# A decoder layer with sparse attention: the DMA issues of the projections in written order, ScalarE's searches served first by VectorE, and tile 2's search held back to the attention

## The chip, the cores and the metric

The kernel runs on one core of a Trainium2 chip. The metric is the device time of one execution in microseconds (us). Engines are named as the profile names them: PE is TensorE (matrix products), PEld its weight loads, DVE is VectorE, ACT is ScalarE, POOL is GpSimd, and SP is the engine whose queue issues all DMAs here.

## What is computed

One decoder layer for 1024 tokens of width 1024, all in f32:

```
mod = silu(c) @ w_mod + b_mod -> shift1, scale1, gate1, shift2, scale2, gate2
h   = x * (1 + scale1) + shift1
q, k, v, u, iq, ik, iw = split(h @ w_in)      # q, k, iq, ik get rotary positions
score[t, s] = sum over 8 indexer heads of iw * relu(iq . ik / 8), s <= t
attn  = for each token: softmax attention over the 256 keys of highest score, 8 heads of 64
pool  = trailing means of u (windows 2, 4, 8, 16) minus u, times w_pool, times pool_scale
x = layer_norm(alpha * x + gate1 * (concat(attn, pool) @ w_o))
h = x * (1 + scale2) + shift2
x = layer_norm(alpha * x + gate2 * swiglu(h))
```

## The kernel before

The tokens are eight tiles of 128 (tile i holds tokens 128 i to 128 i + 127). The matrix products of the projections split each f32 operand into a high and a low part and take three products (`SPLITS`), so every weight block is loaded raw (`raw_R`, three slots), copied by ACT (high part), and subtracted by POOL or DVE (low part) into `ws_W`.

The work runs in stages, one after the other on PE:

- **Index projection** (up to 82 us in the profile): iq, ik.
- **Score stage** (82 to 182 us): for tiles 2 to 7 PE multiplies (`lg`), ACT takes the relu (`relu_K`), DVE multiplies by iw and adds (`score_X`). The q projection's products (`pj`) are pieces put between them. Its results get their rotary positions on POOL in a ring of three buffers (`rope_V`) and are stored to memory (`q_d`).
- **u, k and v projections** (182 to 371 us), 24 groups of 24 products (`pair`, `pj`). Among the first eight groups stand the remaining four rows of the modulation: 16 loads of 1 MB (`mset_K`, three buffers), products with `silb` (`md`), a copy by ACT into `macc_V`, and `mod_fin`, which sums it (`gt`, `mc`). The two `macc_V` buffers lie over the ring `rope_V`, so the first copy waits until the last q tile has been stored. The gate's bias and sum lie in `grow`, one half row at a time.
- **Attention** (371 to 524 us): units of a pair of heads and a tile, tiles from 7 down to 0. PE makes the logits (`s`), DVE adds the mask of the search and takes the maximum in one pass (`sm_H` from `s` and `score_X`), ACT takes the exponential, POOL normalises, PE transposes (`pT`) and multiplies by v (`o`).
- **Output projection, feed-forward and second norm** (524 us to the end).

Which 256 keys a token takes is found by a **search** by bits over the scores: 15 passes over the high 16 bits, 16 passes over the low ones, and a final part that writes the mask over the scores. `bisect` is that search as a generator that yields before each step the engine and an estimated duration. Tiles 5 and 4 together and tile 3 (`TILES_A`) run their passes on ACT, with begin, middle and final part on DVE (`colsA_X`, buffers `junkA_T`, `junkB_X`); tiles 7 and 6 together (`colsD_X`) and tile 2 (`colsE_X`, keys in `keysA_X`, `LATE = [2]`) run on DVE alone. Tile 2's mask is needed when tile 2's first unit is reached, in the third of the four groups of tiles.

Two things set the order. The framework's scheduler may move an instruction ahead of earlier written ones of the same engine, except where `keep_in_program_order` is called on it. The kernel has its own model of the times (`Times`, `Queue`): every instruction goes through a `Queue`, and before an instruction is written whose engine is idle in the model, `fill` writes steps of open searches into the gap. From the first `open_stream` to the end of the v projection the set `pinned` holds V, A and G (DVE, ACT, POOL): these engines keep the written order. SP and PE don't, and in the attention none does. `fill` leaves tile 2 alone as long as the search of tiles 7 and 6 is open, so tile 2's search is written in the attention.

Of the kernel before, what the change touches and what calls it, by code (L numbers as in the profile page):

```python
# [18 lines left out]
ALU = mybir.AluOpType  # L19

P = 128
S = 1024
# [14 lines left out]
TILES_A = [[3], [5, 4]]  # L37
# [7 lines left out]
LATE = [2]  # L45
# [28 lines left out]
def f_(ap):  # L74

    return ap.bitcast(F32)
# [54 lines left out]
class Queue:  # L131
# [24 lines left out]
    def __getattr__(self, op):  # L156
        f = getattr(self.eng, op)

        def call(*a, **k):
            tm = self.times  # L160
            aps = [x for x in list(a) + list(k.values()) if hasattr(x, "tensor")]
            outs = aps[:1] + ([k["accum_out"]] if "accum_out" in k else []) + ([a[-1]] if op == "tensor_tensor_reduce" else [])
            ins = aps[1:]
            if self.name == "S":
                at = tm.ready("S", outs, ins)
                tm.dma = max(tm.dma, at) + outs[0].nbytes() / 320e3
                tm.done("S", outs, ins, tm.dma + 2.0)
                return f(*a, **k)
            if tm.fill is not None:
                tm.fill(self, tm.ready(self.name, outs, ins))  # L170
            ins_ = f(*a, **k)  # L171
            if aps:
                at = max(self.t, tm.ready(self.name, outs, ins))
                self.t = at + self.cost(op, aps, k)
                tm.done(self.name, outs, ins, self.t)
            if self.name in self.pinned:
                self.tc.keep_in_program_order(ins_)
            return ins_

        return call  # L180
# [3 lines left out]
def decoder_layer_kernel(  # L184
# [7 lines left out]
    pinned, times = set(), Times()  # L192
    V, A, G, T, SP = (Queue(tc, e, n, pinned, times) for e, n in
                      ((nc.vector, "V"), (nc.scalar, "A"), (nc.gpsimd, "G"), (nc.tensor, "T"), (nc.sync, "S")))
# [13 lines left out]
    def buf(where, off, n, name, dt=F32):  # L208
        return nc.alloc_sbuf_tensor_at(f"{name}_{where}{off}", [P, n], dt, offset=area[where] + 4 * off).ap()
# [13 lines left out]
    def psA(nm="pa"):  # L223
        return ps_tile(ps1, "ps1", 512, 4, nm)
# [44 lines left out]
    def raw_slot():  # L269
        n_raw[0] += 1  # L270
        return RAW[(n_raw[0] - 1) % 3]

    def split(dst, raw, n, lo_eng=None):
        A.activation(dst[:, 0:n], raw, AF.Copy)
        (lo_eng or V).tensor_tensor(dst[:, n : 2 * n], raw, f_(dst[:, 0:n]), ALU.subtract)
# [140 lines left out]
    def q_flush(keep):  # L416
        while len(q_spill) > keep:
            t, raw = q_spill.pop(0)
            SP.dma_start(q_d[t], raw)
# [10 lines left out]
    gate_d = [tc.dram_tile([1, 1024], F32, name=f"gate{q}_d") for q in range(2)]  # L430
# [228 lines left out]
    streams = []  # L659

    def open_stream(*a):
        pinned.update(PIN)
        b = bisect(*a)
        streams.insert(0, [T.t, next(b), b, a[0]])
        times.fill = fill

    def start(st):
        return max(st[0], queues[st[1][0]].t)

    def advance(st):  # L670
        fill, times.fill = times.fill, None
        q = queues[st[1][0]]
        try:
            st[1] = next(st[2])
        except StopIteration:
            streams.remove(st)
        st[0] = q.t
        times.fill = fill

    def need(i):  # L680
# [3 lines left out]
    def fill(q, until):  # L684
        while True:

            first = [st for st in streams if 7 in st[3]]
            todo = [st for st in streams if not (first and st[3] == LATE) and st[1][0] == q.name and start(st) + st[1][1] <= until + SLACK.get(q.name, 0.0)]
            if not todo:
                return  # L690
            advance(min(todo, key=start))


    n_rr = [0]
# [2 lines left out]
    def q_piece():  # L697
        if not qt[2]:
            if qt[0] >= NT:
                return  # L700
            qt[1], qt[2] = proj_pieces(qt[0])
        qt[2].pop(0)()
        if not qt[2]:
            qpend.append((qt[0], qt[1]))
            qt[0] += 1

    for i in range(2, NT):
# [3 lines left out]
        n = P * (i + 1)  # L711
# [33 lines left out]
    wps = buf("X", 7552, 1024, "wps", F32R)  # L745
# [63 lines left out]
        A.activation(vst[t // 4][:, t % 4], v3(pp), AF.Copy)  # L809

    MSET = [buf("K", 2048 + i * 2048, 2048, "mset") for i in range(3)]
    silb = buf("X", 5312, 256, "silb")
    grow = buf("X", 5568, 512, "grow")
    macc = [buf("V", 5616 + i * 512, 512, "macc") for i in range(2)]
    m_ps = {}

# [18 lines left out]
    def mod_fin(s_):  # L835

        row, c = divmod(s_, 2)
        acc = macc[s_ % 2]
        if row in (0, 3):
            pm = psA("gt")  # L840
            T.matmul(pm, ones, acc, start=True, stop=True)
            V.tensor_tensor(grow[0:1, :], grow[0:1, :], pm[0:1, :], ALU.add)
            SP.dma_start(gate_d[row // 3][:, c * 512 : (c + 1) * 512], grow[0:1, :])
            if s_ != 7:
                n = {0: 1, 1: 6, 6: 7}[s_]
                SP.dma_start(grow[0:1, :], bg_in[n // 6 : n // 6 + 1, n % 2 * 512 : n % 2 * 512 + 512])
        else:
            pc = psA("mc")
            for j in range(4):
                T.matmul(pc[:, j : j + 1], acc[:, j * P : (j + 1) * P], ones[:, 0:1], start=True, stop=True)  # L850
            u = (row - 1) * 8 + c * 4
            V.tensor_tensor(m2[:, u : u + 4], pc[:, 0:4], bcol[:, 16 + u : 20 + u], ALU.add)
            if s_ == 5:
                V.scalar_tensor_tensor(h2c[:, 0:8], m2[:, 8:16], 1.0, lnc[:, 0:8], ALU.add, ALU.mult)
                V.scalar_tensor_tensor(h2c[:, 8:16], m2[:, 8:16], 1.0, lnc[:, 8:16], ALU.add, ALU.mult)
                V.tensor_tensor(h2c[:, 8:16], h2c[:, 8:16], m2[:, 0:8], ALU.add)

    def w_loads(w_in):
        for kp in range(3):
            raws[kp] = raw_slot()  # L860
            SP.dma_start(raws[kp], w_in[kp])
        raws[3] = w_in
# [10 lines left out]
    def at_(slot, f):  # L873
        late.setdefault(slot, []).append(f)

    while qt[2] or qt[0] < NT:
        q_piece()
    w_loads(wu_in)
    for h in range(3):
        mod_load(h)  # L880
    SP.dma_start(lnc, lncol_in)
    SP.dma_start(grow[0:1, :], bg_in[0:1, 0:512])
    V.tensor_copy(silb.rearrange("p (k r) -> p k r", r=32), silc.unsqueeze(2).to_broadcast([P, 8, 32]))
    for i in range(4):
        G.memset(ub[i][:, 0:16], 0.0)
# [4 lines left out]
        q_evac(*qpend.pop(0))  # L890
    wp_raw = raw_slot()
    SP.dma_start(wp_raw[:, 0:512], wpool_in)
    split(wps, wp_raw[:, 0:512], 512)
    at_(1, lambda: q_flush(0))

    def u_f(g, c):
        return lambda pp, ks: mm_k(pp, lambda k, b: ww(k, b, g * P, P), lambda k, a: hh(k, a, c * 512, 512), ks)
# [11 lines left out]
    held, pair = {}, None  # L909
    for n_, (kind, a, b) in enumerate(groups):  # L910
        if n_ in PAIRS:
            pb = psB("pair")
            held[n_], held[n_ + 1] = pb[:, 0:512], pb[:, 512:1024]
            pair = [(held[q_], u_f(*groups[q_][1:]) if kind == "u" else t_f(groups[q_][1])) for q_ in (n_, n_ + 1)]
        if n_ in held:
            for kp in range(2):
                for pp, f in pair:
                    f(pp, [4 * (n_ not in PAIRS) + 2 * kp, 4 * (n_ not in PAIRS) + 2 * kp + 1])
        else:
            held[n_] = psA("pj")  # L920
            (u_f(a, b) if kind == "u" else t_f(a))(held[n_], range(KT))
        pp = held[n_]
        if n_ in (6, 14):
            w_loads(wk_in if n_ == 6 else wv_in)
        if n_ in (7, 8, 15, 16):
            for kp in ((0, 1) if n_ % 2 else (2, 3)):
                w_split(kp)
        nd = n_ + 2 if n_ in PAIRS else n_ + 1
        if kind == "u":
            at_(nd, lambda a=a, b=b, pp=pp: u_take(a, b, pp))  # L930
            if b == 1:
                at_(nd + 1, lambda a=a: u_split(a))
                at_(nd + 1, lambda a=a: u_split2(a))
                at_(nd + POOL_AT, lambda a=a: u_pool(a))
        elif kind == "k":
            tr = n_ + (4 if n_ in PAIRS or n_ - 1 in PAIRS else 3)
            at_(nd, lambda a=a, pp=pp, tr=tr: take(a, pp, tr))
        else:
            at_(nd, lambda a=a, pp=pp: v_take(a, pp))
        if n_ == 20:  # L940
            SP.dma_start(GR, gate_d[0].to_broadcast([P, 1024]))
        q_ = n_ - MOD_AT
        if 0 <= q_ < 9:
            if q_:
                mod_fin(q_ - 1)
            if q_ < 8:
                mod_half(2 * q_)
        for f in late.pop(n_, []):
            f()
        if 0 <= q_ < 8:  # L950
            mod_half(2 * q_ + 1)
# [777 lines left out]
    for p in range(1, NFP):  # L1729
        n_of = {"g": 0, "d": 0, "u": 0}  # L1730
        for kind in DOWN_AT if p < NFP - 1 else "g" * 7 + "u" * 7:
            n = n_of[kind]
# [133 lines left out]
```

## Time and profile before

| what | value |
|---|---|
| runs | 1308.19, 1311.80, 1307.18 us; median 1308.19 |
| profiled execution | 1309.66 us; its span 1307.9 us, granted clock 0.964 |
| PE busy | 1211.9 us (93%) |
| DVE busy | 1001.6 us (77%) |
| ACT busy | 650.4 us (50%) |
| POOL busy | 718.7 us (55%) |

The shares are means over stages with different limits. The span begins with the first instruction that the profiler sees; the execution's own time holds 1.8 us more. In the rows below a time in square brackets is how long the engine stood idle before the instruction, with what ended the wait; "x16" is a count of instructions that stand behind one another; L171 is the line of the `Queue` helper through which nearly all instructions pass, so rows are told apart by tiles.

### The profile page before, as it was taken

To read this page: it belongs to the slowest core of one execution; us is meant where nothing else is said; L and a number is where in the kernel's file an instruction comes from. 1 tells how busy PE (TensorE), PEld (TensorE's weight loads), DVE (VectorE), ACT (ScalarE), POOL (GpSimd) and SP (SyncE) were. 2 spreads that over 40 slices of the span, in tenths; PEclk is the share of its full clock that TensorE was granted. 3 is DMA by queue.
4 is the path that set the end of the run, shared out by engine and by line. 5 is a ranking of instruction groups with operands and counts; after the bars stand their busy time and mean duration, and the time that the engine had idled before them with its cause. 6 is when DMAs were issued, how large, how long until landed. Compare 5 with 4: busy or idle time off the path is not lost.

```text
span 1307.9 us, 16418 instructions
## 1 busy us (share of the span) xinstructions
PE 1211.9 (93%) x5622; PEld 936.8 (72%) x5622; DVE 1001.6 (77%) x1846; ACT 650.4 (50%) x1343; POOL 718.7 (55%) x509
## 2 busy tenths in 40 slices
PE   7979895999988899998789999999999999999996
PEld 5755563677865566887678787878788787878775
DVE  6769999799847666567797777776878777777698
ACT  3346784665897888356534333333424333333531
POOL 1382263467313246237767475574838475576848
PEclk8989998999988999999799999999999999999999
DMA  9510043740100015500121111212010111203112
GB/s 350 196 68 17 17 161 126 267 171 30 44 17 9 9 41 178 177 9 10 54 75 33 65 65 33 81 33 81 33 65 33 65 65 33 81 33 114 49 58 119
DMA packets 32468, 103.40 MB, mean 79 GB/s; under 512 B 3577, under 2 KB 3577, under 8 KB 28801
## 3 DMA queue, kind: packets, MB, share of 16 engines
q1 hardware_dynamic: 32384, 102.36, 22.4%
q8 instruction: 44, 0.72, 0.2%
q14 instruction: 40, 0.32, 0.1%
HBM read 92.90 MB, written 9.45 MB: 78 GB/s over the span
## 4 chain that ended last, share of the span: by engine, by line
PE 55%; DVE 24%; ACT 7%; POOL 6%; issue 6%; DMA 1%; SPq 0%; DVEq 0%; POOLq 0%; ACTq 0%
PE gu L171 24%; PE dn L171 14%; DVE junk_X L171 4%; PE wo L171 4%; DVE score_X L171 4%; PE pj L171 3%; PE s L171 2%; DVE act_W L171 2%; PE pair L171 2%; PE pT L171 2%; PE o L171 2%; POOL wraw_R L171 2%; DVE stat_C L171 1%; DVE utmp_X L171 1%; DVE hr_H L171 1%
## 5 line engine op out<-in xcount | busy, mean ns | idle before, releaser
L171 PE MATMUL gu<-hr_H,wblk_T 128*128 128x512 f32 (+1 forms) x924 | 218.3, 389 | 4.9 <-POOL wblk_T L171 1.9
L171 PE MATMUL gu<-hr_H,wblk_V 128*128 128x512 f32 (+1 forms) x924 | 215.1, 384 | 3.7 <-POOL wblk_V L171 1.9
L171 PEld LDWEIGHTS gu<-hr_H,wblk_T 128*128 128x128 f32 x924 | 173.0, 192 | 41.5 <-POOL wblk_T L171 3.6
L171 PEld LDWEIGHTS gu<-hr_H,wblk_V 128*128 128x128 f32 x924 | 170.0, 188 | 40.0 <-POOL wblk_V L171 3.6
L171 DVE TENSOR_TENSOR res_X<-res_X,dn 128x512 f32<-128x512 f32 (+1 forms) x253 | 159.0, 678 | 15.4 <-PE dn L171 15.3
L171 PE MATMUL pj<-ws_W,hT_H 128*128 128x512 f32 x456 | 118.4, 409 | 7.2 <-POOL ws_W L171 5.1
L171 POOL TENSOR_TENSOR wraw_R<-wraw_R 128x512 f32<-128x512 f32 x64 | 94.7, 1487 | 47.0 <-DVE wblk_T L171 23.7
L171 POOL TENSOR_TENSOR wraw_W<-wraw_W 128x512 f32<-128x512 f32 x60 | 86.6, 1452 | 57.9 <-DVE wblk_V L171 29.3
L171 POOL TENSOR_SCALAR sm_H<-sm_H,stat_X 128x1024 f32<-128x1024 f32 (+7 forms) x64 | 49.7, 791 | 116.7 <-DVE stat_X L171 106.1
L171 PEld LDWEIGHTS pj<-ws_W,hT_H 128*128 128x128 f32 x456 | 85.7, 194 | 32.1 <-issue 6.8
L171 PE MATMUL dn<-wblk_T,act_W 128*128 128x512 f32 x324 | 79.6, 394 | 4.5 <-DVE act_W L171 4.5
L171 PE MATMUL dn<-wblk_V,act_W 128*128 128x512 f32 x324 | 78.5, 391 | 2.9 <-DVE act_W L171 2.5
L171 DVE TENSOR_SCALAR_CACHE_REDUCE junk_X<-keysD_T,colsD_X 128x1024 int16<-128x1024 int16 (+1 forms) x64 | 78.9, 1267 | 0.2
L171 ACT ACTIVATE wblk_V<-wraw_R 128x512 fp32r<-128x512 f32 x56 | 35.2, 629 | 80.6 <-POOL wraw_R L171 62.2
L171 PEld LDWEIGHTS dn<-wblk_T,act_W 128*128 128x128 f32 x324 | 60.8, 189 | 19.2 <-DVE act_W L171 6.6
L171 POOL TENSOR_TENSOR ws_W<-raw_R,ws_W 128x1024 fp32r<-128x1024 f32 x17 | 44.6, 2643 | 53.8 <-ACT ws_W L171 53.8
L171 PEld LDWEIGHTS dn<-wblk_V,act_W 128*128 128x128 f32 x324 | 60.4, 188 | 17.4 <-DVE act_W L171 4.2
L171 ACT ACTIVATE wblk_V<-wraw_W 128x512 fp32r<-128x512 f32 x53 | 33.1, 627 | 75.0 <-POOL wraw_W L171 56.4
L171 ACT ACTIVATE wblk_T<-wraw_W 128x512 fp32r<-128x512 f32 x56 | 35.0, 628 | 66.3 <-POOL wraw_W L171 50.2
L171 ACT ACTIVATE wblk_T<-wraw_R 128x512 fp32r<-128x512 f32 x52 | 32.5, 627 | 61.0 <-POOL wraw_R L171 45.6
L171 ACT ACTIVATE junkA_T<-keys_T,colsA_X 128x768 bf16<-128x768 uint16 (+3 forms) x62 | 54.3, 876 | 5.8 <-DVE colsA_X L171 5.2
L171 ACT ACTIVATE utmp_X<-gu 128x512 f32<-128x512 f32 x33 | 19.7, 598 | 73.4 <-PE gu L171 73.4
(295 smaller groups left out, 2769.5 us busy)
## 6 DMA issues: line engine op xcount, KB each, us to landing
mset_K<-in_wmr_dram SPq DMA_DIRECT2D x16, 1024.0 KB, 6.0
wm_K<-in_wma_dram SPq DMA_DIRECT2D x16, 512.0 KB, 9.7
wraw_R<-in_wg_dram SPq DMA_DIRECT2D x6, 1024.0 KB, 4.8
wraw_R<-in_wd_dram SPq DMA_DIRECT2D x12, 512.0 KB, 3.5
wraw_W<-in_wup_dram SPq DMA_DIRECT2D x12, 512.0 KB, 3.6
wraw_R<-in_wup_dram SPq DMA_DIRECT2D x10, 512.0 KB, 3.8
wraw_W<-in_wg_dram SPq DMA_DIRECT2D x5, 1024.0 KB
wraw_W<-in_wd_dram SPq DMA_DIRECT2D x10, 512.0 KB, 3.6
```

The source lines that it names most:

```text
L171: ins_ = f(*a, **k)
```

## The change

It has three parts that touch the same stages.

1. **SP in written order.** `Queue` calls `keep_in_program_order` on DMAs too, and `"S"` is added to `pinned` after the last q piece, until the end of the v projection. With it the written order is changed: all q stores stand ahead of the modulation's later loads (`q_flush(0)` at once, no longer in a later slot), the loads of wk and wv stand four groups earlier (`n_ in (2, 10)`), the low part of the pooling weights (`wps`) is subtracted by POOL and no longer by DVE, and the gate's row is loaded, summed and stored whole (`grow` of 1024, two stores and two loads in place of four and four; `silb` moves to another area to make room).
2. **Order among searches.** Where DVE could serve several open searches at the same time, those of ACT's tiles (`TILES_A`) come first.
3. **Tile 2 held.** The first step of tile 2's search, when it is written after `pinned` was cleared, is itself kept in program order on DVE. The steps behind it depend on it.

```
 Queue, DMA branch
-                return f(*a, **k)
+                ins_ = f(*a, **k)
+                if self.name in self.pinned:
+                    self.tc.keep_in_program_order(ins_)
+                return ins_
 open_stream
-        streams.insert(0, [T.t, next(b), b, a[0]])
+        streams.insert(0, [T.t, next(b), b, a[0], True])
 advance
+        held = st[3] == LATE and st[4] and "V" not in pinned
+        st[4] = False
+        if held:
+            pinned.add("V")
         ...
+        if held:
+            pinned.discard("V")
 fill
-            advance(min(todo, key=start))
+            advance(min(todo, key=lambda st: (start(st), st[3] not in TILES_A)))
 mod_fin, gate rows
-            V.tensor_tensor(grow[0:1, :], grow[0:1, :], pm[0:1, :], ALU.add)
-            SP.dma_start(gate_d[row // 3][:, c * 512 : (c + 1) * 512], grow[0:1, :])
-            if s_ != 7:
-                n = {0: 1, 1: 6, 6: 7}[s_]
-                SP.dma_start(grow[0:1, :], bg_in[n // 6 : n // 6 + 1, n % 2 * 512 : n % 2 * 512 + 512])
+            gc = grow[0:1, c * 512 : (c + 1) * 512]
+            V.tensor_tensor(gc, gc, pm[0:1, :], ALU.add)
 ...
+        if s_ in (3, 7):
+            SP.dma_start(gate_d[s_ // 4], grow[0:1, :])
+        if s_ == 3:
+            SP.dma_start(grow[0:1, :], bg_in[1:2, :])
 projections
+    pinned.add("S")
     w_loads(wu_in)
 ...
-    split(wps, wp_raw[:, 0:512], 512)
-    at_(1, lambda: q_flush(0))
+    split(wps, wp_raw[:, 0:512], 512, G)
+    q_flush(0)
 ...
-        if n_ in (6, 14):
-            w_loads(wk_in if n_ == 6 else wv_in)
+        if n_ in (2, 10):
+            w_loads(wk_in if n_ == 2 else wv_in)
```

How it moves instructions, at three places. First SP, at the start of the u projection: `raw_R` are the weight slots, `in_wk_dram` the k weights, `mset_K` the modulation's buffers, `q_d` the stores of q. Before:

```order
L168 DMA raw_R_75<-in_wu_dram 128x1024
L168 DMA raw_R_73<-in_wpool_dram 128x512
L168 DMA raw_R_74<-in_wk_dram 128x1024
L168 DMA raw_R_75<-in_wk_dram 128x1024
L168 DMA q_d<-rope_V_450 128x512
L168 DMA raw_R_73<-in_wk_dram 128x1024
L168 DMA mset_K_1221<-in_wmr_dram 128x2048
L168 DMA q_d<-rope_V_450 128x512
L168 DMA mset_K_1222<-in_wmr_dram 128x2048
```

and now:

```order
L168 DMA raw_R_75<-in_wu_dram 128x1024
L168 DMA q_d<-rope_V_450 128x512 x2
L168 DMA raw_R_73<-in_wpool_dram 128x512
L168 DMA q_d<-rope_V_450 128x512 x2
L168 DMA mset_K_1221<-in_wmr_dram 128x2048
L168 DMA mset_K_1222<-in_wmr_dram 128x2048
L168 DMA raw_R_74<-in_wk_dram 128x1024
L168 DMA raw_R_75<-in_wk_dram 128x1024
L168 DMA raw_R_73<-in_wk_dram 128x1024
L168 DMA mset_K_1223<-in_wmr_dram 128x2048
```

The last q store moved ahead of the three loads of k weights and of one load of the modulation.

Second DVE in the score stage, at tile 3's scores (128x512); `colsE_X` marks tile 2's search, `ql_V` the low part of the next tile's index queries, for which PE waits. Before:

```order
L171 SCALAR_TENSOR_TENSOR score_X_77<-relu_K_557,const_C_78,score_X_77 128x512
L171 TENSOR_SCALAR junk_X_608,colsE_X_610<-score_X_77 128x384
L171 TENSOR_SCALAR colsE_X_610<-colsE_X_610 128x1 x4
L171 SCALAR_TENSOR_TENSOR score_X_77<-relu_K_557,const_C_78,score_X_77 128x512
L171 TENSOR_TENSOR keysA_X_599<-score_X_77,colsE_X_610 128x384
L171 SCALAR_TENSOR_TENSOR score_X_77<-relu_K_557,const_C_78,score_X_77 128x512
L171 TENSOR_SCALAR junk_X_608,colsE_X_610<-keysA_X_599,colsE_X_610 128x384
L171 TENSOR_SCALAR colsE_X_610<-colsE_X_610 128x1 x2
```

and now:

```order
L174 TENSOR_SCALAR score_X_77<-relu_K_557,const_C_78 128x512
L174 SCALAR_TENSOR_TENSOR score_X_77<-relu_K_557,const_C_78,score_X_77 128x512 x3
L174 TENSOR_TENSOR ql_V_449<-qT_723,qa_K_556 64x512 x2
L174 SCALAR_TENSOR_TENSOR score_X_77<-relu_K_557,const_C_78,score_X_77 128x512 x4
L174 TENSOR_SCALAR junkB_X_607,colsA_X_600<-score_X_77 128x512
```

Tile 2's search has left the score stage; in between, the rows that stay keep their order.

Third DVE in the attention, between masks of tile 7 (`sm_H` 128x1024) and tile 6 (128x896). Before, where the final part of tiles 5 and 4 begins:

```order
L171 ISA sm_H_2642,stat_X_2637<-s_2942,score_X_77 128x1024
L171 ISA stat_X_2637 128x1
L171 TENSOR_SCALAR colsA_X_600<-colsA_X_600 128x2
L171 CAST colsA_X_600<-colsA_X_600 128x2
L171 TENSOR_TENSOR colsA_X_600<-colsA_X_600 128x2 x2
L171 TENSOR_SCALAR keys_T_605<-score_X_77,colsA_X_600 128x768
L171 TENSOR_SCALAR junkA_T_606,colsA_X_600<-score_X_77,colsA_X_600 128x768
```

and now, two units earlier in the same group:

```order
L174 ISA sm_H_2671,stat_X_2666<-s_2816,score_X_77 128x1024
L174 ISA stat_X_2666 128x1
L174 TENSOR_SCALAR colsE_X_610<-colsE_X_610 128x1
L174 RECIPROCAL stat_X_2666<-stat_X_2666 128x2
L174 TENSOR_SCALAR junk_X_608,colsE_X_610<-keysA_X_599,colsE_X_610 128x384
L174 TENSOR_SCALAR colsE_X_610<-colsE_X_610 128x1
L174 COPY pT_H_2668<-pT_2883 128x4x128
L174 TENSOR_SCALAR colsE_X_610<-colsE_X_610 128x1
```

The final part of tiles 5 and 4 now stands ahead of the first mask, and passes of tile 2 stand between the masks: in the whole order, 10 of tile 2's 34 passes over keys or scores stand ahead of the first mask and 24 between the first and the 24th, where all 34 stood ahead of the first before. On ACT, 5 passes of tiles 5 and 4 (of 62 instructions) and 15 of tile 3 (of 31) stood behind the first exponential before; now none and 7. From the second half of tiles 5 and 4's units on, the orders of all engines are the same up to a few neighbours that change places.

More of the change, by code (lines that the diff above doesn't have):

```diff
@@ L811, in decoder_layer_kernel @@
     MSET = [buf("K", 2048 + i * 2048, 2048, "mset") for i in range(3)]
-    silb = buf("X", 5312, 256, "silb")
-    grow = buf("X", 5568, 512, "grow")
+    silb = buf("V", 5168, 256, "silb")
+    grow = buf("X", 5312, 1024, "grow")
     macc = [buf("V", 5616 + i * 512, 512, "macc") for i in range(2)]
@@ L881, in decoder_layer_kernel @@
     SP.dma_start(lnc, lncol_in)
-    SP.dma_start(grow[0:1, :], bg_in[0:1, 0:512])
+    SP.dma_start(grow[0:1, :], bg_in[0:1, :])
     V.tensor_copy(silb.rearrange("p (k r) -> p k r", r=32), silc.unsqueeze(2).to_broadcast([P, 8, 32]))
```

## The prediction

> **What bounds the kernel now.** I read the table of stretches first, one row for each stage the change touches: score, the first groups of u, the rest of u, k and v, and attention. Columns: stretch and its length, then busy time and count of PE, PEld, DVE, ACT and POOL, the granted clock, the DMA share and GB/s.
>
> ```profile
> 82.00:182.00 100.00, 91.38 (x361) 58.08 (x361) 85.79 (x182) 64.00 (x114) 38.78 (x35) 0.96 0.12 43
> 182.00:224.00 42.00, 30.79 (x133) 19.84 (x133) 40.84 (x106) 25.70 (x73) 23.76 (x15) 0.88 0.42 157
> 375.00:397.00 22.00, 19.00 (x67) 11.25 (x66) 12.91 (x24) 21.91 (x53) 6.44 (x6) 0.77 0.00 1
> 375.00:457.00 82.00, 71.06 (x373) 45.28 (x372) 56.95 (x115) 70.46 (x177) 23.93 (x22) 0.88 0.03 7
> ```
>
> PE sets the end: it is busy for 93% of the span and in each of these stages bar the second the fullest or next to it. What can be gained is its idle time and the time in which its clock is low. The second row stands out: in 42 us PE works 30.79, and DVE 40.84, 97%. The third and fourth rows are the first half of attention: ACT is full at first (21.91 of 22), DVE has room. Next I read what DVE does in the first two stretches, by the tile of tile 2's search (columns: stretch, DVE's busy time of this tile alone, clock, DMA share, GB/s), and PE's own rows in order of time:
>
> ```profile
> 80.00:180.00 100.00, 23.90 (x94) 0.95 0.11 38
> 180.00:224.00 44.00, 16.82 (x50) 0.88 0.43 161
> ...
> 195.97 5.71 PE L171 MATMUL pj<-hT_H,ws_W 128*128 128x512 f32 x24
> ...
> 212.74 2.08 PE L171 MATMUL gt<-macc_V,const_C 128*128 128x512 f32 x2 [9.93 <-ACT macc_V L171]
> 214.74 2.51 PE L171 MATMUL md<-mset_K,silb_X 128*32 128x512 f32 x16
> 224.73 1.10 PE L171 MATMUL gt<-macc_V,const_C 128*128 128x512 f32 x2 [1.81 <-DVE grow_X L171]
> 229.78 1.93 PE L171 MATMUL md<-mset_K,silb_X 128*32 128x512 f32 x8 [2.49 <-DMA mset_K<-in_wmr_dram]
> 231.64 6.36 PE L171 MATMUL pj<-hT_H,ws_W 128*128 128x512 f32 x24
> ```
>
> So tile 2 takes 40.7 us of DVE, whose result is not needed for another 200 us, and PE stands for 14.23 us (9.93 + 1.81 + 2.49) just there. The chain behind the 9.93:
>
> ```profile
> 204.05 0.69 DVE L171 TENSOR_TENSOR wps_X<-raw_R,wps_X 128x512 fp32r<-128x512 f32 x1
> 204.77 0.33 SPq L168 DMA_DIRECT2D raw_R<-in_wk_dram  x1
> 205.19 0.38 SPq L168 DMA_DIRECT2D mset_K<-in_wmr_dram  x1
> 205.66 0.38 SPq L168 DMA_DIRECT2D q_d<-rope_V  x1
> 212.09 0.60 ACT L171 ACTIVATE macc_V<-md 128x512 f32<-128x512 f32 x1 [12.94 <-DMA q_d<-rope_V]
> ```
>
> DVE, busy with tile 2, reaches the low part of `wps` at 204.05. That frees the weight slot for which a k load waits at the head of SP's queue; it is issued at 204.77, a modulation load at 205.19, and only then the last q store. The store keeps ACT from overwriting the ring, and PE from its `gt`, until 212.7.
>
> **The u projection: 15 us gained.** The first stall goes twice over: the store stands ahead of the k loads, and POOL does `wps`. Late next are POOL's last rotary piece and the modulation's loads:
>
> ```profile
> 198.43 1.30 POOL L171 TENSOR_TENSOR rope_V<-rope_V,ptmp_C 128x512 f32<-128x512 f32 x1
> ...
> q_d<-rope_V SPq DMA_DIRECT2D x8, 256.0 KB, 2.2
> mset_K<-in_wmr_dram SPq DMA_DIRECT2D x16, 1024.0 KB, 6.0
> ```
>
> The piece ends at 199.73; with 2.2 for the store and 0.60 for ACT's copy `macc_V` is there at 202.5. PE reaches that point at 195.97 + 5.71 = 201.7, so a wait of 0.8 stays. In SP's written order the third modulation buffer's next load can't go before that last store, so it is issued about 200.1 and lands 6.0 later, at 206.1. PE, with one group of products less to wait behind, would want it about 204.6 (201.7, the 0.8, and 2.1 for `gt`): 1.5 more. The 1.81 of `grow` goes, since its add at 223.91 (below) stood behind tile 2's final part, and the 2.49 because later loads no longer stand behind k loads that wait for slots. The halves of `grow` stored together, two stores and two loads fewer, cost SP nothing: four issues of 0.38 in a queue that waits anyway. `wps` on POOL is about 1.3 (the rotary piece has the same 128x512) of POOL's time, which is 57% busy in this stretch, hidden under PE's groups of 5.7; without that cover it would delay the k weights' low part by as much.
>
> Behind the stalls PE also runs slower. The same products later in the same stage:
>
> ```profile
> 240.57 5.75 PE L171 MATMUL pj<-hT_H,ws_W 128*128 128x512 f32 x24
> ...
> 257.07 1.92 PE L171 MATMUL md<-mset_K,silb_X 128*32 128x512 f32 x16
> 265.39 1.06 PE L171 MATMUL md<-mset_K,silb_X 128*32 128x512 f32 x8
> 274.54 1.02 PE L171 MATMUL gt<-macc_V,const_C 128*128 128x512 f32 x2
> ```
>
> 2.08 against 1.02, 2.51 against 1.92, 1.93 against 1.06, 6.36 against 5.75: together 3.13 us, which go with the stalls. The sum is 14.23 + 3.13 - 2.3 = 15.1. Its ends: 17.4 if the new waits are hidden, 5.4 if two modulation loads, 6.0 each, come late by their whole landing. I stay near the upper end since both waits I can name are worked out from rows.
>
> **The score stage: 6 us gained.** Here nothing is added; DVE only loses the 94 instructions of tile 2. PE's waits in this stage, and an example of what follows one:
>
> ```profile
> PE lg L171 <- ACT relu_K L171: 4.6, 9, 1.9
> PE lg L171 <- DVE ql_V L171: 3.6, 6, 1.4
> ...
> 163.11 1.67 PE L171 MATMUL pj<-ws_W,hT_H 128*128 128x512 f32 x6
> 166.70 0.73 PE L171 MATMUL lg<-ikE_K,qa_K 128*128 128x512 f32 x2 [1.92 <-ACT relu_K L171]
> 169.77 2.49 PE L171 MATMUL pj<-ws_W,hT_H 128*128 128x512 f32 x6
> ```
>
> The first two give 8.2 in all (total, times, longest): ACT waits for buffers that DVE frees, DVE brings `ql_V` late. After the wait of 1.92 the same six products took 2.49 in place of 1.67, 0.8 more. The most is thus 9.0, the least 0, where ACT's own work (64 of 100) holds the relu. DVE without tile 2 has 62 of 100 to do, so I take two thirds, 6.
>
> [...]
>
> **Attention: 1 us lost.** Both searches on ACT end sooner. ACT's share of them in the first half and DVE's part of tiles 5 and 4's final part (of `colsA_X`, DVE then ACT), and tile 2's passes:
>
> ```profile
> 375.00:457.00 82.00, 11.45 (x23) 28.93 (x85) 0.88 0.03 7
> ...
> 398.88 0.16 DVE L171 TENSOR_SCALAR colsA_X<-colsA_X 128x2 f32<-128x2 f32 x1
> 415.22 0.48 DVE L171 TENSOR_SCALAR score_X<-junkA_T 128x640 f32<-128x640 bf16 x1
> ...
> L171 DVE TENSOR_SCALAR_CACHE_REDUCE junk_X<-keysA_X,colsE_X x32: 660/672/675, 107.1 to 212.8; 128x384 int16<-128x384 int16 x16, 128x384 uint16<-128x384 uint16 x16
> L171 DVE DVE_READ_ACCUMULATOR junk_X<-keysA_X,colsE_X x32: 77/83/91, 107.7 to 213.4; 128x1 f32 x32
> 213.72 0.40 DVE L171 TENSOR_SCALAR colsE_X<-colsE_X 128x1 f32<-128x1 f32 x2
> 223.91 0.68 DVE L171 TENSOR_TENSOR grow_X<-grow_X,gt 1x512 f32<-1x512 f32 x1
> ```
>
> ACT: of 20 searching instructions behind the first exponential 7 stay, so its 28.93 falls to about 10 and its 70.46 to about 52: it no longer binds. DVE: 56.95, less the final part of tiles 5 and 4, which moves ahead of the first mask. That part is 16.8 us from its first row to the end of its last, of which I estimate 13 its own (two masks and small copies stand between). Added are 24 passes of 0.672 + 0.083 + 0.40 = 1.155 each, 27.7; the middle part, one pass and small ones, 1.5; and the final part, from 214.1 to 223.9, 9.8. 56.95 - 13 + 27.7 + 1.5 + 9.8 = 83, in a stretch of 82. DVE takes ACT's place as the bound, and the stretch is about as long: -1. PE's transposes wait for DVE's copies in DVE's queue, and behind each mask now stand one or two passes. The ends: if DVE keeps the 9.1 idle of the first 22 us (22.00 - 12.91), 10 are lost; if the passes fit into gaps that PE doesn't see, half of what PE lacks there, 10.9 idle and 8.5 by the clock of 0.88, is gained, 10. The final part of tiles 5 and 4 goes to the v projection, where ACT's earlier end must be early enough; the steps of tiles 5 and 4 are served first there, for which DVE had 40.7 us freed.
>
> One more stall lies near the moved loads, ahead of a v product:
>
> ```profile
> 324.49 7.15 PE L171 MATMUL pair<-ws_W,hT_H 128*128 128x512 f32 x23 [2.34 <-POOL ws_W L171]
> ```
>
> It names POOL's splitting, not the load, so it stays in my sum. From the output projection on nothing moves.
>
> **Sum.** 15.1 + 6 - 1 = 20.1 less than the profiled execution's 1309.66 (span 1307.9 and 1.8 around it): 1289.6. That execution lies 1.47 above the median of the runs, so on the median's basis 1288.
>
> **Rivals.** *Attention gains too.* ACT filled the first 22 us there, at a clock of 0.77, and that load is what the change takes away. If PE's waits were ACT's more than DVE's, the +10 end holds: 1288 - 11 = 1277. Against it: PE's waits name DVE's `stat_X` and `ws_W`, and DVE gets more to do.
>
> *The written order of SP makes new waits.* A store that waits for POOL now holds back loads of weights and modulation behind it. With the 5.4 end of the u projection: 1288 + 9.7 = 1298.
>
> *Nothing is left of it.* The 5.4 end and the loss of 9 more in attention together: 1288 + 9.7 + 9 = 1307, no change that can be told. The same comes out if the order changes but PE's stalls only get other names.
>
> *Slower: tile 2 comes onto the path.* The 24 passes, the middle and final part, 27.7 + 1.5 + 9.8 = 39 us, move from where DVE was full but PE could partly run on to a place where each step stands between a mask and PE's next logits. Were all of it on the path while the other 21 are gained, the time would be 1308.2 - 21.1 + 39 = 1326. This decides for slower once more than 21.1 + 6.5 = 28 of the 39 are not hidden. Against it: DVE has 25 us free in the 82, so at least that much should be hidden.
>
> **How the numbers follow.** The forecast, 1281 to 1295, gets 55%; attention gaining, 1272 to 1281, 20%, and 2% still lower; new waits, 1295 to 1301.7, 13%; no change, 6%; tile 2 on the path, 4%. About 0.5% (6.5 us) is what a measurement of this kernel can tell from no change. Faster by more than that is thus 0.90, within it 0.06, slower 0.04. The range of 8 in 10 leaves out no change, slower, and the outer parts of the two neighbours: 1273 to 1300.
>
> **What the profile after would show.** In the u projection: the last q store issued about 200 and ahead of the k loads, `gt` with less than 2 idle where it had 9.93, and its clock above 0.93. In the score stage: PE's waits on `relu_K` and `ql_V` at 3 or less in place of 8.2. In attention: DVE near 80 of 82, ACT near 52, PE waiting more often for DVE than now. It would be wrong by the first rival if the stretch from the first to the 24th mask is shorter by over 5, by the second if PE waits for `mset_K` or `ws_W` for over 8 between 182 and 260, by the slower one if it stands before masks of tile 2 or between passes for over 28.

## The result and the profile after

The changed kernel takes 1293.24 us (median; 1292.83 to 1293.41) beside 1308.83 of the kernel before: ratio 0.9877, 95% interval 0.9864 to 0.989. The forecast was 1288, its range 1273 to 1300. So the time came out 5 us above the forecast and inside its range. The reason did not come out: the runs below show that the first part of the change, to which the prediction gave most of the gain, makes the kernel 4.9 us slower by itself; that the gain of the score and u stages comes with the hold of tile 2; and that without the tie-break, which the prediction hardly priced, the stages behind take all of it back. That the sum came near was luck in part: the score stage gained 3.8 more than forecast, u gained 2.0 less, and the attention with its entry lost 4.1 more.

Where PE stands at the ends of the stages, from PE's rows in order of time (us):

| PE reaches | before | after | gain in this stage |
|---|---|---|---|
| first `lg` | 86.74 | 87.00 | -0.3 |
| end of the last `lg` (score) | 174.47 | 164.89 | 9.8 |
| end of the last `gt` (u projection) | 283.95 | 261.25 | 13.1 |
| end of `qT` (k and v projections) | 372.08 | 349.52 | -0.1 |
| first `s` (entry into attention) | 373.66 | 358.28 | -7.2 |
| last `s` (attention) | 519.66 | 502.15 | 2.1 |
| end of the last `dn` | 1296.49 | 1279.98 | -1.0 |

The stretches of these stages, first before, then after (stretch and length; busy time and count of PE, PEld, DVE, ACT, POOL; clock; DMA share; GB/s). The last row of each goes from the first mask to the 24th.

```profile
82.00:175.00 93.00, 84.42 (x332) 52.66 (x333) 79.13 (x173) 58.36 (x103) 33.02 (x28) 0.96 0.07 26
175.00:284.00 109.00, 94.52 (x450) 61.36 (x449) 95.15 (x225) 72.14 (x186) 59.89 (x38) 0.92 0.58 212
...
375.77:456.20 80.43, 69.48 (x364) 44.23 (x365) 55.48 (x112) 69.23 (x174) 23.93 (x22) 0.87 0.03 7
```

```profile
82.00:165.00 83.00, 79.79 (x330) 51.56 (x331) 63.21 (x79) 57.14 (x103) 34.24 (x27) 0.96 0.07 26
165.00:262.00 97.00, 93.13 (x454) 60.57 (x455) 82.35 (x186) 75.98 (x197) 63.59 (x40) 1.00 0.61 225
...
350.00:365.54 15.54, 3.33 (x7) 2.14 (x8) 13.94 (x48) 13.38 (x31) 0.00 (x0) 0.64 0.11 34
365.54:439.61 74.07, 67.38 (x369) 44.72 (x368) 65.67 (x196) 52.02 (x115) 22.21 (x22) 0.84 0.03 8
```

In the score and u stages PE is now 96% busy. The row 350.00:365.54 is new: 15.5 us in which PE works 3.33 while DVE works 13.94 and ACT 13.38. PE's rows after, in u and at that entry:

```profile
187.59 5.60 PE L174 MATMUL pj<-hT_H,ws_W 128*128 128x512 f32 x24
194.67 1.12 PE L174 MATMUL gt<-macc_V,const_C 128*128 128x512 f32 x2 [1.47 <-ACT macc_V L174]
195.72 1.06 PE L174 MATMUL md<-mset_K,silb_V 128*32 128x512 f32 x8
197.14 1.06 PE L174 MATMUL md<-mset_K,silb_V 128*32 128x512 f32 x8 [0.35 <-DMA mset_K<-in_wmr_dram]
198.14 5.78 PE L174 MATMUL pj<-hT_H,ws_W 128*128 128x512 f32 x24
203.75 1.02 PE L174 MATMUL gt<-macc_V,const_C 128*128 128x512 f32 x2
...
358.28 2.08 PE L174 MATMUL s<-kr_K,qab_H 128*128 128x512 f32 x4 [8.76 <-ACT qab_H L174]
...
364.29 1.94 PE L174 MATMUL s<-kr_K,qab_H 64*128 64x512 f32 x4 [3.93 <-DVE qab_H L174]
```

The 14.23 us of stalls in u have become 1.82 (1.47 + 0.35). Beside them PE waits 2.0 in all for POOL's `ws_W`, where it waited 0.2 before. At the entry PE waits 8.76 for ACT's copies of `qab_H`, and 3.93 for their low part from DVE. What ACT and DVE did ahead of them:

```profile
344.41 0.72 ACT L174 ACTIVATE junkB_X<-keysA_X,colsA_X 128x512 bf16<-128x512 uint16 x1 [6.00 <-DVE colsA_X L174]
...
356.45 2.40 ACT L174 ACTIVATE qab_H<-qT 64x512 fp32r<-64x512 f32 x4
...
362.83 0.67 DVE L174 TENSOR_SCALAR_CACHE_REDUCE junk_X<-keysA_X,colsE_X 128x384 int16<-128x384 int16 x1
...
363.55 1.41 DVE L174 TENSOR_TENSOR qab_H<-qT,qab_H 64x512 fp32r<-64x512 f32 x2
```

ACT stood idle for 6.00 until DVE had made tile 3's middle part, then ran eight of tile 3's passes, and only behind them, at 356.45, copied the q operands that had been ready since 349.5. DVE has held tile 2's passes since 352: ten of them stand ahead of the subtraction at 363.55.

### The profile page after: what moved, and what is told of

Its sections match the earlier page's. It is cut to its first block, busy times and chain, and to the rows that moved or that the text cites. A ratio compares the mean times of both kernels' runs of the same rounds, so it can differ in the third digit from the quotient of the medians.

```text
span 1291.6 us, 16411 instructions
## 1 busy us (share of the span) xinstructions
PE 1200.3 (93%) x5622; PEld 932.2 (72%) x5622; DVE 994.8 (77%) x1845; ACT 654.5 (51%) x1343; POOL 722.5 (56%) x510
## 4 chain that ended last, share of the span: by engine, by line
PE 60%; DVE 18%; POOL 9%; issue 7%; ACT 5%; DMA 1%; SPq 0%; DVEq 0%; POOLq 0%; ACTq 0%
PE gu L174 24%; PE dn L174 14%; PE pj L174 5%; PE wo L174 4%; PE pair L174 3%; PE s L174 2%; PE pT L174 2%; PE o L174 2%; DVE act_W L174 2%; DVE score_X L174 2%; POOL wraw_R L174 2%; DVE junk_X L174 2%; PE lg L174 2%; DVE utmp_X L174 1%; POOL ws_W L174 1%
## 5 line engine op out<-in xcount | busy, mean ns | idle before, releaser
L174 ACT ACTIVATE sm_H<-sm_H,stat_X 128x1024 f32<-128x1024 f32 (+7 forms) x64 | 49.1, 771 | 16.7 <-DVE stat_X L174 16.5
```

## The experiments

**The three parts, alone and in pairs.** Part 1 is SP's order (with `wps` on POOL and the gate rows whole), part 2 the tie-break, part 3 the hold of tile 2. Each edit takes the text of the other parts back to the kernel before.

Part 1 alone:

```
-            advance(min(todo, key=lambda st: (start(st), st[3] not in TILES_A)))
+            advance(min(todo, key=start))
-        held = st[3] == LATE and st[4] and "V" not in pinned
+        held = False
```

> Part 1 alone (SP in written order with the moved issues, wps on POOL, gate rows whole); no tie-break, tile 2 not held. Theory A (the gains lie in separate stages, and the 10 us stall in u is SP's order): the score stage ends as before (last lg at 174 to 175), the wait of gt for macc_V falls from 9.9 to under 3, about 1296 to 1299. Rival B (the stall is only DVE's fullness with tile 2, whatever SP's order): the stall stays over 6, time 1304 to 1309.

Measured: 1314.34 beside 1309.45 (1.0032, 1.002 to 1.0045): slower. Both theories missed. The wait for `macc_V` did fall to 2.0, but the time did not go with it:

```profile
204.03 1.12 PE L174 MATMUL gt<-macc_V,const_C 128*128 128x512 f32 x2 [2.01 <-ACT macc_V L174]
205.08 1.07 PE L174 MATMUL md<-mset_K,silb_V 128*32 128x512 f32 x8
207.86 1.06 PE L174 MATMUL md<-mset_K,silb_V 128*32 128x512 f32 x8 [1.71 <-DMA mset_K<-in_wmr_dram]
208.85 5.74 PE L174 MATMUL pj<-hT_H,ws_W 128*128 128x512 f32 x24
219.16 2.05 PE L174 MATMUL gt<-macc_V,const_C 128*128 128x512 f32 x2 [4.57 <-issue]
221.13 1.94 PE L174 MATMUL md<-mset_K,silb_V 128*32 128x512 f32 x8
228.17 4.64 PE L174 MATMUL pj<-hT_H,ws_W 128*128 128x512 f32 x10 [5.10 <-DVE grow_X L174]
```

PE reaches the second `gt` some eight us earlier and stands for 4.57 and 5.10 instead. The second time it waits for DVE's add into `grow`. For the first the profile names nothing ("issue"), but the add into `grow` ahead of it, which stands behind tile 2's final part on DVE, ends at 219.05, just before `gt` starts at 219.16; the later add, of 227.45, stands behind passes of tiles 7 and 6. The u stage is 1.2 longer than before. The stall had only got other names. Another 6.3 go in k and v, 2.7 of them in a wait for DVE's `kr_K` that the kernel before does not have.

Part 2 alone (in the kernel before, `key=start` is replaced by the new key):

> Part 2 alone. Theory A3: score and u as before (last lg 174 to 175, gt near 284); the gap between ACT's high and low bits of tiles 5 and 4 falls from 44 to under 12; attention 8 to 12 shorter after its first logits, of which an entry wait of 7 to 10 is given back: 1302 to 1307. Rival B3 (without tile 2 held DVE has no room to serve ACT): 1307 to 1311.

Measured: 1313.89 beside 1309.03 (1.0034, 1.0022 to 1.0045): slower, outside both. Score and u were as before (174.75; 284), and attention behind its first logits was 7.6 shorter, but the entry cost 10.5: PE stood 12.0 for ACT's `qab_H`. The gap between ACT's high and low bits of tiles 5 and 4, from start to start, fell from 44 to 14, not under 12.

Part 3 alone (the `held` lines of the change in the kernel before):

> Part 3 alone (tile 2 held in attention), SP and ties as before; on DVE only. Theory A: the last lg comes 9 to 10 earlier than before's 174.5; the q store still stands behind the k loads, but wps is no longer late on DVE, so gt's wait of 9.9 falls by half or more; no long wait of PE for qab_H by ACT at the start of attention; 1293 to 1299. Rival B (only the score stage gains, DVE's passes are lost again in attention): 1300 to 1306.

Measured: 1302.10 (0.9956, 0.9931 to 0.998). The score stage gains 10.0 and u 13.7, with SP's order as before: `gt` waits 2.1 for `macc_V`. So u's gain belongs to DVE's freedom from tile 2 and not to the DMA order. Attention gives 17.8 of it back, so the time is rival B's, though not its mechanism: B had no gain in u. PE's rows there:

```profile
348.77 1.35 PE L171 MATMUL s<-kr_K,qab_H 128*128 128x512 f32 x4 [1.57 <-ACT qab_H L171]
362.30 1.94 PE L171 MATMUL s<-kr_K,qab_H 64*128 64x512 f32 x4 [12.17 <-DVE qab_H L171]
```

Parts 1 and 2, without the hold (`held = False` in the changed kernel):

> All but part 3: tile 2 not held, so its passes go back to the score stage. Theory A: the score stage ends 9 to 10 later than with all three (last lg near 174.5 in place of 164.9), u keeps its short waits, PE's first logits no longer wait 3.9 for DVE; 1298 to 1303. Rival B (tile 2 takes as much in attention as it did in the score stage): within 3 of the changed kernel's 1293.

Measured: 1305.67 (0.9965, 0.9954 to 0.9976). The last `lg` ends at 174.17 and u's last `gt` at 285.3: without the hold both gains are gone. The time lies 3 above A's range, because u too was lost. From PE's first `s` to its last, attention takes 134.8, where it is 146.0 before and 143.9 with all three: held, tile 2 costs 9 there, out of the 24.6 that it saves in score and u.

Parts 1 and 3, without the tie-break (`key=start` in the changed kernel):

> All but part 2: among searches that could be served at the same time the old order. Theory A: score and u as with all three; ACT's searches end later, so the final part of tiles 5 and 4 stays in attention; PE's wait for ACT's first qab_H (8.8 with all three) is gone or under 3, the rest of attention is longer; in all 1288 to 1292. Rival B (ACT bounds attention, the tie-break is what pays there): 1297 to 1303.

Measured: 1308.70 (0.9996, 0.9984 to 1.0008): the whole gain is gone, more than either theory said. Score and u gain as with all three (24.1 to the last `gt`), then k and v lose 5.0 (2.7 of them in the wait for `kr_K` that part 1 alone showed) and attention 17.8, with a wait of 13.5 for DVE's `qab_H`. What the tie-break changes is seen on ACT, here without it: the last pass of tiles 5 and 4 over the high bits, the first over the low ones, and DVE's passes for tiles 7 and 6 in the 55 us between (times: least, median, most in ns; first and last start):

```profile
231.45 0.83 ACT L174 ACTIVATE junkA_T<-keys_T,colsA_X 128x640 bf16<-128x640 int16 x1
...
287.39 0.94 ACT L174 ACTIVATE junkA_T<-keys_T,colsA_X 128x768 bf16<-128x768 uint16 x1 [0.36 <-DVE colsA_X L174]
...
L174 DVE TENSOR_SCALAR_CACHE_REDUCE junk_X<-keysD_T,colsD_X x24: 1190/1262/1339, 231.7 to 283.9; 128x1024 uint16<-128x1024 uint16 x10, 128x896 uint16<-128x896 uint16 x10, 128x1024 int16<-128x1024 int16 x2, 128x896 int16<-128x896 int16 x2
```

and with it:

```profile
232.13 0.83 ACT L174 ACTIVATE junkA_T<-keys_T,colsA_X 128x640 bf16<-128x640 int16 x1
...
240.62 0.92 ACT L174 ACTIVATE junkA_T<-keys_T,colsA_X 128x768 bf16<-128x768 uint16 x1
...
L174 DVE TENSOR_SCALAR_CACHE_REDUCE junk_X<-keysD_T,colsD_X x2: 1206/1272/1337, 238.7 to 239.9; 128x1024 int16<-128x1024 int16 x1, 128x896 int16<-128x896 int16 x1
```

A middle part of a few us on DVE waited behind 24 passes of another search; now behind two. ACT's low bits begin 47 us earlier, and the final part of tiles 5 and 4 leaves the attention (their masks are written at 342 and 350 in place of 407 and 416).

Parts 2 and 3, without SP's order (the kernel before with the new key and the `held` lines):

> All but part 1: tile 2 held and the tie-break, SP's order, wps on DVE and the gate's halves as before. Theory A2 (new, after the first runs: u's 13 us come from DVE having no tile 2 there, and SP's order is worth nothing): gt's last end 22 to 24 earlier than before, as with all three, and the time 1290 to 1296. Rival B2 (SP's order is what keeps the tie-break's gain, since k's products waited without it): 1299 to 1304.

Measured: 1298.88 (0.9921, 0.9897 to 0.9944), between the two. u gains 14.4, no less than with SP's order; the stages behind it are worse by 10 than with all three in the profiled execution, which is 2.7 slower than the median: the entry (10.5 lost in place of 7.2) and attention (2.9 lost in place of 2.1 gained) most of all. Tiles 5 and 4's high bits end at 248 on ACT in place of 233. So beside the other two, part 1 is worth 5.6 us (1298.88 - 1293.24), and not by way of PE's stall in u. That it works by way of ACT's searches is what these rows suggest; no run tries it.

Over the eight combinations, score and u together are 23.0 to 24.3 shorter than before in the four with the hold, and between 0.3 shorter and 1.6 longer in the three others that were changed.

**Which half of part 1.** The changed kernel with the low part of `wps` on DVE:

```
-    split(wps, wp_raw[:, 0:512], 512, G)
+    split(wps, wp_raw[:, 0:512], 512)
```

> All three parts, but the low part of wps on DVE as before, SP's order left as changed. Theory A3 (what part 1 is worth beside the other two, 1298.9 to 1293.2, comes from SP's order, by which ACT no longer stands 4.2 for the last q store): 1292 to 1295. Rival B3 (it comes from wps having left DVE): 1297 to 1300.

Measured: 1294.61 (0.9893, 0.9876 to 0.991), the same as the changed kernel within the intervals. So it isn't `wps`; that leaves SP's order with the moved issues, and the whole gate rows, which were not tried apart.

**Which half of the tie-break.** All three parts, but of ACT's searches the middle part goes first and the final part does not (`yield "V", ..., 1` marks the steps of the middle part; the marked lines are also passed at the end of the low bits, ahead of a few small steps that open the final part, and by the middle parts of DVE's own searches):

```
-            advance(min(todo, key=lambda st: (start(st), st[3] not in TILES_A)))
+            advance(min(todo, key=lambda st: (start(st), len(st[1]) < 3)))
```

> All three parts, but the tie-break narrowed to one step: only the middle part of ACT's searches (after the high bits) goes first where DVE could serve several; their final parts don't. Theory A3 (the tie-break pays because tiles 5 and 4's middle part waited 44 to 56 us on DVE between ACT's high and low bits): that gap stays under 12, and the time is 1290 to 1296. Rival B3 (it pays by the earlier final parts on DVE): 1300 to 1308.

Measured: 1288.33 (0.9833, 0.9811 to 0.9855): the gap is 8.5 from start to start, and the time is even below A3's range. The middle part is all that the tie-break has to serve; to put the final part of tiles 5 and 4 ahead as well costs 4.9 (1293.24 - 1288.33).

**The entry.** Tile 2 not before the first mask is written:

```
-            todo = [... if not (first and st[3] == LATE) and ...]
+            todo = [... if not ((first or not n_st[0]) and st[3] == LATE) and ...]
```

> All three parts, and tile 2 may not be served before the first mask is written, so its ten passes leave the place ahead of DVE's low part of the first qab_H. Theory A2: PE's wait of 3.9 for DVE's qab_H goes; the ten passes (11.5 us of DVE) go to where DVE is the bound and cost about as much again: 1290 to 1298. Rival B2 (DVE has gaps there that PE doesn't see): 1287 to 1290.

Measured: 1290.66 (0.9859, 0.9842 to 0.9876). The wait of 3.93 is gone, and first to 24th mask take 73.9 beside 74.1. But of the 10.0 us that DVE spent on tile 2 ahead of the first mask only 2.9 more lie between these masks (31.25 beside 28.32); 6.3 lie behind the 24th. From PE's first `s` to its last, attention is 3.0 shorter (140.9 beside 143.9), so of the 3.93 about one is felt again. DVE had gaps there that PE doesn't see: rival B2's mechanism holds, though the time lies 0.66 above its range and inside A2's.

Tile 3's first low pass kept in written order on ACT:

```
+        heldA = st[3] == [3] and st[1][0] == "A" and "A" not in pinned and not holdA
+        if heldA:
+            holdA.append(1)
+            pinned.add("A")
 ...
+        if heldA:
+            pinned.discard("A")
```

> All three parts, and tile 3's first pass of the low bits is kept in written order on ACT, so seven of its passes stand behind the copies of qab in place of ahead of them. Theory A2: PE's 8.8 for ACT's qab_H falls to under 2, but the low part of qab_H still stands behind tile 2's ten passes on DVE, so PE's second products start within 2 of where they did: 1291 to 1295. Rival B2 (ACT's queue is the whole of the entry's price): 1284 to 1287.

Measured: 1299.47 (0.9925, 0.9908 to 0.9941), slower than the changed kernel; both missed. ACT's wait fell to 1.5, but the wait for DVE's `qab_H` rose to 10.8, as A2 said, and the passes of tile 3 (eight, not seven) came back between the masks, which A2 had not priced: first to 24th mask 82.6 in place of 74.1.

Both edits:

> Both of these edits on top of all three parts. Theory A2: the entry's waits go from 12.7 to about 2, PE's first logits come 9 to 11 earlier; 11.5 us of DVE's passes and 10 of ACT's come back between the masks, where half of it is felt: 1285 to 1290. Rival B2 (nothing is felt): 1280 to 1284; rival C2 (all of it is): 1292 to 1296.

Measured: 1290.50 (0.9856, 0.9841 to 0.9871), between A2 and C2. The first mask comes 7.8 earlier than with the first edit alone, and the masks take 8.6 longer (82.5 to 73.9). Between these masks now also lies all of tile 2's work; over all of attention, where that makes no difference, it is 8.4 longer (149.3 to 140.9). So the eight passes on ACT cost about the same on either side of the entry, and I took it that not their place had to change but the 6.00 that ACT waits before them.

So the last kernel makes them start earlier: DVE stays in written order until the first q operands are made, and middle parts (marked as above) go first among ties, so that tile 3's stands ahead of tile 4's scan and the final part of tiles 7 and 6; tile 2 as in the first of these edits.

```
     pinned.clear()
+    pinned.add('V')
 ...
         q_make(i, qr[i], qp[i])
+    pinned.discard('V')
 ...
-            advance(min(todo, key=lambda st: (start(st), st[3] not in TILES_A)))
+            advance(min(todo, key=lambda st: (start(st), st[3] not in TILES_A, len(st[1]) < 3)))
```

> The kernel with tile 2 after the first mask, and DVE kept in written order until the first qab is made, with the middle parts first among ties: tile 3's middle part stands ahead of tile 4's scan and of the final part of tiles 7 and 6. Theory A3: ACT's idle 6.0 ahead of tile 3's low bits goes, PE's wait of 8.8 for ACT's qab_H falls to under 4; 1284 to 1288. Rival B3 (the freed ACT time is filled by more of tile 3's passes ahead of qab_H): 1289 to 1292.

Measured: 1282.99 (0.9795, 0.9778 to 0.9813), faster than both kernels and 1 below A3's range. ACT's low bits of tile 3 begin at 337.5 (344.4 with the change), and PE waits 5.0, not 8.76 and 3.93:

```profile
353.21 3.75 PE L174 MATMUL s<-kr_K,qab_H 128*128 128x512 f32 x8 [5.00 <-ACT qab_H L174]
...
356.47:427.76 71.29, 63.88 (x368) 40.98 (x366) 65.10 (x210) 53.21 (x114) 22.13 (x22) 0.89 0.03 9
```

ACT's wait was not gone (4.1 in place of 6.0) and PE's not under 4, so both signs of A3 were missed; the gain came in part from the masks, 71.3 from first to 24th, with 7.6 of tile 2's work on DVE behind the 24th. What the written order of DVE and the new key bring apart was not tried.

## Why the prediction was right or wrong

- **Score, 6 forecast, 9.8 measured.** Right cause: part 3 alone gives 10.0. PE's waits for `relu_K` and `ql_V` went from 8.2 to 3.0, nearly as forecast. The term that was too small is PE's slower running behind the waits, 0.8: from the first `lg` to the end of the last, PE's busy time fell from 79.41 to 74.82 at 320 products each, 4.6. 5.2 + 4.6 = 9.8, more than the 9.0 that the prediction had as the most. One example of slow clock (granted 0.50 from 168.19 to 171.61 before) was taken for the whole of the term, and the clock is the smaller part of it: its mean over these stretches is 0.98 before and 0.99 after, worth some 1 us by my estimate (0.02 of 87.7 less 0.01 of 77.9). 2.9 of the 4.6 lie in the products that read `ql_V`, whose busy time fell from 20.98 to 18.04 for 80 each. Of the 80, 26 start within 0.02 of the one ahead before, and 31 after. One pair, before and after: where DVE brought `ql_V` late (waits of 0.95 and 0.23), the second product started 0.73 behind the first; without a wait both start at 136.98:

```profile
140.78 0.49 PE L171 MATMUL lg<-ikE_K,ql_V 64*128 64x512 f32 x1 [0.95 <-DVE ql_V L171]
141.51 0.50 PE L171 MATMUL lg<-ikO_K,ql_V 64*128 64x512 f32 x1 [0.23 <-DVE ql_V L171]
...
136.98 0.50 PE L174 MATMUL lg<-ikE_K,ql_V 64*128 64x512 f32 x1
136.98 0.49 PE L174 MATMUL lg<-ikO_K,ql_V 64*128 64x512 f32 x1
```

- **u, 15.1 forecast, 13.1 measured.** The size is nearly right (new waits 1.82 for 2.3; most of the 2.0 that are missing is the wait for POOL's `ws_W`, which I did not have), the cause is not. "The first stall goes twice over: the store stands ahead of the k loads, and POOL does `wps`" failed: with both, and tile 2 still on DVE, nothing is gained (part 1 alone, -1.2), and without both, 13.7 is (part 3 alone). The chain quoted began with DVE, which held `wps` back until 204.05; I cut it at SP. With tile 2 in place PE runs into DVE's next late results, the two adds into `grow`: waits of 4.57 and 5.10 where there was one of 1.81. Of that one I had the cause right: it stands behind tile 2's final part and goes when that goes.
- **Attention, -1 forecast, -5.1 measured**, in two parts of opposite sign. ACT's busy time between the masks fell to 52.02, as forecast. DVE's did not rise to 83: 65.67. Two terms of that sum were off. Tile 2 took 28.32 there, not 39, in part since its final part was priced by 9.8 of elapsed time from a stretch in which single steps took up to 2.27; in part 1 alone the same steps take 4.3 in all (214.10 to 218.35). And what left weighs 18 (55.48 + 28.32 - 65.67), not 13. DVE did not become the bound, and the stretch is 6.4 shorter, past the 5 that I had named as the first rival's sign. Given back is the entry, 7.2 (11.1 with the 3.93, which the table counts to the attention), which I had at nothing: ACT's earlier end "must be early enough" was a condition left without a price. For tiles 5 and 4 it holds (342 to 350 is before the entry); what fails is tile 3, whose middle part now stands behind steps of their final part and of that of tiles 7 and 6.
- **Tie-break.** I gave it no term of its own. Without it the other two parts together leave 1308.7: no change. Alone it loses. The parts do not add up: 4.9 and 4.9 slower, 7.3 faster alone, 15.6 faster together.
- **The rest** was forecast unchanged, and is, within 1 us.
- **The clock.** 3.13 of u's 15.1 were slower running behind the stalls. The granted clock is now 1.00 from 165 to 262, where it was 0.92 from 175 to 284, and behind idles of 1.47 and 0.35 `gt` and `md` take 1.12 and 1.06, where they took 2.08 and 1.93 behind 9.93 and 2.49. In part 1 alone `md` and `gt` took 1.06 and 1.12 behind 1.71 and 2.01; behind 4.57 and 5.10 `gt` took 2.05 and ten `pj` 4.64, where the changed kernel's take 1.02 (at 203.75) and 2.60 (at 205.70). But not every slow product goes with the stall just ahead of it. Before, the granted clock is 0.50 from 168.19 to 171.61 and from 226.22 to 233.05: it fell 1.5 us after the wait of 1.92 in the score stage had ended, and before the one of 2.49 in u began. What makes it fall was not tried.

## What to carry to other kernels

Ask of each stall which engine is late at the root, not which queue passes it on: in part 1 alone, with tile 2 still on DVE, the reordered DMAs brought the wait of 9.93 down to 2.01, and PE stood for 4.57 and 5.10 at DVE's next results instead. When searches or other long work share an engine with short steps for which another engine stands idle, serve those steps first; here, without the tie-break, one middle part of a few us held ACT's work back for 55. And when a change ends something sooner, price what stands next in the same engine's order: the passes that ACT and DVE had put ahead of the first q operands took 11 of the 23 us that had been gained (7.2 and 3.9).

## What the runs showed that I had not expected

Eight passes of about 1.5 us on ACT cost PE 7 to 9 us whether they stood ahead of the first logits or between the masks, though without them ACT was busy for only 52 of 74 us there; why ACT's spare time didn't hide them was not tried. And in the score stage a late operand cost PE more than the wait that the profile shows: the products behind it lost their overlap, 2.9 us in all by their busy time, part of it at the slow clock (granted 0.50, 168.19 to 171.61). What is left of the 4.6 stays open.
